# Weight-block sums moved from GpSimd instructions to accumulating DRAM-to-DRAM transfers, and some stores moved to ScalarE's queue

## The chip, the core and the metric

The kernel runs on one core of a Trainium2 chip. A core has five engines that each work through an instruction queue of their own, in order: TensorE (PE: matrix products into PSUM, with its weight loads PEld), VectorE (DVE), ScalarE (ACT), GpSimd (POOL) and SyncE (SP, which here only issues transfers). They meet through semaphores. Sixteen DMA engines move the data; a transfer is issued by an instruction on SP's, ACT's or POOL's queue. The metric is the device time of one execution in microseconds (us), lower is better.

## What is computed

One layer of a hybrid diffusion backbone in float32 over 1024 latent tokens of width 1024, with 256 context tokens. Cut to what matters here:

```python
hx = modulate(rmsnorm(x, norm1_g), sh1, sc1)
xq, xk, xv, xrq, xrk, xrv, xrg, xga, xgb = split(hx @ w_in)
o_na  = neighbourhood_attention(...)            # 8 heads of 64
o_ret = ret_output(bi_retention(...), xrg)      # 4 heads, chunks of 128, both directions
merged = sigmoid(xga) * (o_na @ w_proj_na) + sigmoid(xgb) * (o_ret @ w_proj_ret)
x = x + g1 * (merged @ w_out)
hx2 = modulate(rmsnorm(x, norm2_g), sh2, sc2)
u = depthwise_conv3(hx2 @ w_up) + conv_b        # w_up: 1024 x 5632
a, val = split(u)
x = x + g2 * ((silu(a) * val) @ w_down)         # w_down: 2816 x 1024
return rmsnorm(x, final_norm_g)
```

## The kernel before

Every float32 product is made of three TensorE products of halves: an operand is split into a rounded part (ACT, L86) and the rest (DVE, L87), and high*high, high*low and low*high are added in PSUM. So each weight block of 128x512 that arrives from DRAM passes through one ACT and one DVE instruction before TensorE may use it. The stages follow each other: start, neighbourhood attention (32 units, with pieces of projections and five plain gates between them), retention (4 heads of 10 slots, with three more plain gates at the end), the projection of the attention, the gates, `pret`, the output projection, the gated MLP's first product ("up"), its second ("down").

The gates, up and down are made by a scheme with seven block products in place of eight (class `Seven`, L1371 to L1431, and the loops of down). It needs sums and differences of the four 128x512 weight blocks of a unit, called s1 to s4. Three such sets exist:

- Gates and up: `Seven.load` (L1379) loads four blocks a21, a22, a11, a12 and lets POOL make s1 to s4 by four instructions (L1383 to L1386). In the up stage these eight tiles share a rotation of 12 buffers (`ur_load`, L1733; an earlier user of the same buffers is `comb`, which loads 16 tiles of the activation's sums). There are 22 up units; the first two are made plainly, the other 20 by the scheme. Unit i's seven steps are interleaved with its neighbours' (L1435): a unit takes seven steps' time, a step is 12 matmuls.
- Down: `down_sums` (L1238) is a generator that loads four w_down blocks on SP's queue into SBUF, subtracts on POOL (L1249) and stores the results to `d_w` in DRAM on SP's queue. It is advanced one subtraction at a time from the retention's slots, from the gates and from `pret`. 11 sets, 44 subtractions, 44 loads, 44 stores.

In a retention slot POOL also makes the rotated queries and keys (L1115: `r`), the low halves of the states (L1166: `SS`) and a power (L1193: `mvr`); all three feed TensorE by way of other engines. The retention's results leave by SP (`d_oret`, L1210), as do the plain gates (`d_gate`, L361). A store on SP's queue waits there for the ACT copy that fills its tile, and everything behind it on SP waits with it.

The order on each engine is set by the framework's list scheduler except where a part is written out by hand (the start, a piece of down's end); `late(...)` keeps marked instructions in the order of the program.

Of the kernel before, what the change touches and what calls it, by code (L numbers as in the profile page):

```python
# [8 lines left out]
F32 = mybir.dt.float32  # L9
# [7 lines left out]
P = 128  # L17
# [23 lines left out]
def tile_hybrid_layer(ctx, tc: tile.TileContext, io, dbg=None):  # L41
# [24 lines left out]
    edge = sb("edge", "right")  # L66
    cpool.tile([P, 24], F32, name="pad")
    edge.tile([P, 24], F32, name="pad")
# [467 lines left out]
    def ada_col2(i):  # L536
        w = ada2[i]
        late(vec.scalar_tensor_tensor(w, w, 1.0, cs2, ALU.mult, ALU.mult, accum_out=col[:, 16 + i : 17 + i]))  # L538
        if i + 1 < 32:
            ada_load()  # L540


    dec = cpool.tile([P, RH, 6], F32, name="dec")

# [468 lines left out]
    for i in range(NPAIR * NJ + 2):  # L1013
        live = i < NPAIR * NJ
        u1 = us[i - 1] if 1 <= i <= NPAIR * NJ else None
        u2 = us[i - 2] if i >= 2 else None
        if i == 0:
            ada_load()
        for n in (0, 1) if i == 1 else (i,) if 1 < i < 32 else ():
# [46 lines left out]
    class Head:  # L1066
# [129 lines left out]
        def mix_c(self, n):  # L1196
# [12 lines left out]
            if not end:  # L1209
                sync.dma_start(*stores.pop())  # L1210

# [23 lines left out]

    NH = NF // 2

    def down_sums(pool_, j0, j1, bufs=8):  # L1238
        def load(j, n):
            t = pool_.tile([P, 512], F32, tag="pj", bufs=bufs, name="pj")  # L1240
            sync.dma_start(t, io["w_down"][n % 2, NH * (n // 2) + j])
            return t

        ts, store = [load(j0, n) for n in range(4)], None
        yield
        for j in range(j0, j1):
            nxt = []
            for n, (c, x, y, o) in enumerate(((1, 1, 0, 0), (3, 3, 1, 1), (2, 3, 0, 3), (4, 2, 3, 2))):
                late(pool.tensor_tensor(ts[o], ts[x], ts[y], ALU.subtract))  # L1249
                if store:  # L1250
                    sync.dma_start(*store)
                store = (d_w[j, c - 1], ts[o])
                if j + 1 < j1:
                    nxt.append(load(j + 1, n))
                yield
            ts = nxt
        sync.dma_start(*store)

    RET_SUMS, GATE_SUMS = 5, 9
    ret_sums = down_sums(rt, 0, RET_SUMS)  # L1260
# [81 lines left out]
    def hx_sums(k):  # L1342
# [5 lines left out]
        b11, b12, b21, b22 = b[0, 0], b[0, 1], b[1, 0], b[1, 1]  # L1348
        for c, o, x, y in (("T1", b11, b12, b11), ("T3", b12, b22, b12), ("T2", b22, b22, b11), ("T4", b21, b21, b22)):
            late(vec.tensor_tensor(o, x, y, ALU.subtract))  # L1350
        yield
# [24 lines left out]
    class Seven:  # L1376
        loaded = False

        def load(self):  # L1379
# [3 lines left out]
            pool.tensor_tensor(self.s1, self.a21, self.a22, ALU.add)  # L1383
            pool.tensor_tensor(self.s2, self.s1, self.a11, ALU.subtract)
            pool.tensor_tensor(self.s3, self.a11, self.a21, ALU.subtract)
            pool.tensor_tensor(self.s4, self.a12, self.s2, ALU.subtract)  # L1386

# [8 lines left out]

        def add(self, b, half, bank, x):
            vec.tensor_tensor(self.dst(b, half), bank, x, ALU.add)
            self.done(b, half)

        def step(self, n):
# [7 lines left out]
            elif n == 1:  # L1409
                self.prod(self.Y, self.s2, "T2", True, False)  # L1410
                vec.tensor_tensor(self.u2, self.Y, self.p1, ALU.add)
            elif n == 2:
                self.prod(self.Z, self.s1, "T1", True, False)
            elif n == 3:
                self.fetch(1, 1)
                self.prod(self.Y, self.s3, "T3", False, False)
                vec.tensor_tensor(self.u3, self.Y, self.p1, ALU.add)  # L1417
                self.add(1, 1, self.Z, self.u3)
            elif n == 4:
# [3 lines left out]
            elif n == 5:  # L1423
                self.fetch(1, 0)
                self.prod(self.Y, self.a22, "T4", False, True)
                self.add(1, 0, self.Y, self.p1)
            else:
                self.fetch(0, 1)
                self.prod(self.Z, self.s4, "B22", False, True)
                self.add(0, 1, self.Z, self.u2)  # L1430

# [102 lines left out]

    gate_sums = down_sums(gr, RET_SUMS, GATE_SUMS)
    steps = interleaved(0, len(gu))
    n0, fetched = steps.index((len(gu) - 1, 0)), None
    for n, (i, k) in enumerate(steps):
        gu[i].step(k)
        if n % 3 == 1:  # L1540
            next(gate_sums, None)
        if fetched:
            orr_split(*fetched)
            fetched = None
        if n0 - KH - 1 <= n < n0 - 1:
            fetched = orr_load(wpool.tile([P, 512], F32, tag="raw", bufs=3, name="raw"), 0, n - n0 + KH + 1)
        elif n0 < n <= n0 + KH:
            fetched = orr_load(g_raw("orw"), 0, n - n0 - 1 + KH)

    def pret_load(db):  # L1550
        return [wload(io["w_pret"][db, i]) for i in range(2)]

    wp = {0: pret_load(0)}
    for _ in gate_sums:
        pass
    gr.release()
    tg.release()
# [25 lines left out]

    pjp = sb("out_sums", "right")
    out_sums = down_sums(pjp, GATE_SUMS, NH, 7)
    mg = {}

# [23 lines left out]
    for db in range(2, KB):  # L1611
# [4 lines left out]
        for half in range(2):  # L1616
            pret(db, half)
            next(out_sums, None)
    pjp.release()
    wo = {}  # L1620
# [39 lines left out]
    def norm_out(tb, xr):  # L1660
# [24 lines left out]
        (b11, b21), (b12, b22) = [(t[:, : KB // 2], t[:, KB // 2 :]) for t in (vo, vr)]  # L1685
        vec.tensor_tensor(b11, b12, b11, ALU.subtract)
        vec.tensor_tensor(b12, b22, b12, ALU.subtract)
        vec.tensor_tensor(b22, b22, b11, ALU.subtract)
        vec.tensor_tensor(b21, b21, b22, ALU.subtract)
# [64 lines left out]
    def conv(j, gate, value):  # L1754
# [18 lines left out]
        prev = {}  # L1773
        for c, x, y, o in ((S1, a21, a22, ALU.add), (S2, S1, a11, ALU.subtract), (S3, a11, a21, ALU.subtract), (S4, a12, S2, ALU.subtract)):
            x, y = (prev[v] if isinstance(v, int) else v for v in (x, y))
# [58 lines left out]

    seq = [j + NH * i for j in range(NH) for i in range(2)]
    PLAIN = 2

    for n, j in enumerate(seq[:PLAIN]):
# [8 lines left out]
        conv(j, *us2)  # L1847
    units = [Up(n, j) for n, j in enumerate(seq)]
    for i, n in interleaved(PLAIN, NF):
        units[i].step(n)  # L1850
    pu[1].release()
    pu[0].release()
# [84 lines left out]
    for b in range(QB):  # L1937
        pool.tensor_tensor(u2[b], u2[b], gate2[:, gs(1)], ALU.mult)
        pool.tensor_tensor(u2[b], u2[b], rows_of(b, 1), ALU.add)  # L1939

    steps(4, range(NH), True, False)
    for b in range(QB):
        x, z = rows_of(QB + b, 1), dw_tile("x2", NTB)
        part[QB + b, 1] = z
        vec.tensor_tensor(z, banks[0][b], u3[b], ALU.add)
        pool.tensor_tensor(z, z, gate2[:, gs(1)], ALU.mult)
# [140 lines left out]
```

## Time and profile before

| | us |
|---|---|
| three runs | 1764.68, 1762.41, 1764.07 (median 1764.07) |
| span of the profiled execution | 1759.2 |
| busy in it: PE, PEld, DVE, ACT, POOL | 1726.0, 1429.3, 1284.2, 849.2, 539.3 |
| POOL's L1249 (down's subtractions), 44 of them | 62.7 |
| POOL's L1383 to L1386 in up (20 units), 80 of them | 148.6 |

The span runs from the first to the last instruction of one profiled execution; that execution's own device time is not recorded beside it, so the 4.9 us between the span and the runs' median stand for what lies around the span. Busy time is the union of an engine's instructions. A matmul's record is longer than the distance between two starts (0.39 us against 0.23 us), so PE counts as busy where matmuls overlap, and what is idle on PE is a true stop. In the tables of waits a row reads: engine, tile and line that waited, what released it, us in total, how many times, the longest. In a timeline a row reads: start, length, engine, line, operation, output and inputs, count, and in brackets the idle time before it with what ended it.

### The profile page before, as it was taken

The page shows a single profiled execution, that of the slowest core. Times are in us where ns is not written, and L with a number is a line of the kernel's source. Part 1 is how long each engine was busy: PE and PEld are TensorE (multiplying, and loading weights), DVE is VectorE, ACT ScalarE, POOL GpSimd, SP SyncE. Part 2 cuts the span into 40 slices and gives each one's busy share as a digit, 9 for nine tenths or more (in the row PEclk, how much of TensorE's full clock was granted, in tenths as well). Part 3 has the DMA queues.
Part 4 walks back from the last instruction along what each step waited for, and adds up shares of the span by engine and source line. Part 5 has one row for each costly group of instructions (what it writes and reads, how often), then busy time and mean ns, then how long its engine had stood idle before and what let it go on. Part 6 is the DMA issues. An engine that isn't in the chain of part 4 may idle for free.

```text
span 1759.2 us, 24801 instructions
## 1 busy us (share of the span) xinstructions
PE 1726.0 (98%) x8405; PEld 1429.3 (81%) x8405; DVE 1284.2 (73%) x2454; ACT 849.2 (48%) x1826; POOL 539.3 (31%) x455
## 2 busy tenths in 40 slices
PE   8999999999999999999999999989999999999997
PEld 4688988888888888778888888778888888788886
DVE  4778887756776766777665557868899889875755
ACT  5666666653443434443444324534444444554444
POOL 1000000003334343555413300165555655211444
PEclk9999999999999999999999999999999999999999
DMA  9143334342231212677557733733322332586754
GB/s 348 61 130 125 95 117 147 117 133 87 73 108 43 72 42 68 203 238 239 200 199 268 246 143 132 254 108 102 108 90 92 118 120 90 170 296 192 239 162 162
DMA packets 139408, 261.10 MB, mean 148 GB/s; under 512 B 15856, under 2 KB 28304, under 8 KB 139280
## 3 DMA queue, kind: packets, MB, share of 16 engines
q1 hardware_dynamic: 139280, 259.51, 44.3%
q8 instruction: 66, 1.08, 0.3%
q14 instruction: 62, 0.51, 0.1%
HBM read 187.34 MB, written 69.48 MB: 146 GB/s over the span
## 4 chain that ended last, share of the span: by engine, by line
PE 43%; issue 6%; DVE 4%; POOL 3%; DMA 1%; ACT 1%; SPq 0%; POOLq 0%; ACTq 0%; DVEq 0%
PE u L1374 30%; PE y L1374 4%; PE pr L112 2%; PE pr L111 2%; PE pr L110 2%; PE om L122 1%; PE om L121 1%; PE om L123 1%; POOL x L1902 1%; DVE wc L87 0%; DVE b L1350 0%; DVE v L1679 0%; POOL pd L1939 0%; DVE hxT L87 0%; POOL x L1947 0%
## 5 line engine op out<-in xcount | busy, mean ns | idle before, releaser
L1374 PE MATMUL u<-T,wc 128*128 128x512 f32 x960 | 227.1, 392 | 5.1 <-ACT pu L1408 5.1
L1374 PEld LDWEIGHTS u<-T,wc 128*128 128x128 f32 x960 | 180.6, 189 | 45.7 <-ACT pu L1408 7.9
L1374 PE MATMUL y<-wc,ahl 128*128 128x512 f32 x924 | 210.6, 389 | 2.7 <-DVE wc L87 1.8
L1374 PEld LDWEIGHTS y<-wc,ahl 128*128 128x128 f32 x924 | 173.3, 188 | 39.7 <-DVE wc L87 2.5
L87 DVE TENSOR_TENSOR wc<-ur,wc 128x512 fp32r<-128x512 f32 x137 | 122.7, 897 | 65.8 <-ACT wc L86 65.8
L86 ACT CAST wc<-ur 128x512 fp32r<-128x512 f32 x137 | 85.0, 621 | 129.7 <-PE y L1374 72.3
L111 PE MATMUL mm<-low,wc 128*128 128x512 f32 (+1 forms) x328 | 124.0, 378 | 0.0
L1374 PE MATMUL u<-h2a,wc 128*128 128x512 f32 x480 | 112.3, 389 | 0.7 <-DVE pu L1417 0.7
L110 PE MATMUL mm<-hx,wc 128*128 128x512 f32 x264 | 107.4, 407 | 0.2 <-ACT wc L589 0.2
L1374 PEld LDWEIGHTS u<-h2a,wc 128*128 128x128 f32 x480 | 90.0, 188 | 19.8 <-DVE pu L1417 1.2
L112 PE MATMUL mm<-hx,wc 128*128 128x512 f32 x264 | 105.2, 399 | 0.0
L86 ACT CAST wc<-s 128x512 fp32r<-128x512 f32 x80 | 49.7, 623 | 93.2 <-PE u L1374 88.3
L123 PE MATMUL mm<-wc,low 128*128 128x512 f32 (+1 forms) x240 | 91.2, 380 | 0.0
L1374 PE MATMUL u<-hxT,wc 128*128 128x512 f32 x384 | 89.6, 389 | 0.0
L1508 POOL TENSOR_TENSOR col<-col,bcol 128x32 f32<-128x32 f32 x1 | 0.3, 253 | 280.7 <-DVE aw L538 280.7
L87 DVE TENSOR_TENSOR wc<-s,wc 128x512 fp32r<-128x512 f32 x80 | 83.5, 1046 | 3.8 <-ACT wc L86 3.4
L1374 PEld LDWEIGHTS u<-hxT,wc 128*128 128x128 f32 x384 | 72.1, 188 | 14.9
L87 DVE TENSOR_TENSOR wc<-raw,wc 128x512 fp32r<-128x512 f32 x92 | 68.0, 746 | 17.7 <-ACT wc L86 17.7
L121 PE MATMUL mm<-wc,hx 128*128 128x512 f32 x192 | 75.2, 392 | 0.6 <-ACT r L1105 0.6
L122 PE MATMUL mm<-wc,hx 128*128 128x512 f32 x192 | 75.2, 392 | 0.0
L1383 POOL TENSOR_TENSOR s<-ur 128x512 f32<-128x512 f32 x20 | 35.7, 1783 | 126.3 <-DVE wc L87 68.7
L86 ACT CAST wc<-raw 128x512 fp32r<-128x512 f32 x92 | 56.8, 621 | 33.0 <-PE pr L112 6.0
(393 smaller groups left out, 4671.3 us busy)
## 6 DMA issues: line engine op xcount, KB each, us to landing
ur<-in_w_up SPq DMA_DIRECT2D x80, 256.0 KB, 2.9
ur<-d_a SPq DMA_DIRECT2D x77, 256.0 KB, 3.1
aw<-in_w_ada SPq DMA_DIRECT2D x32, 512.0 KB, 3.3
pj<-in_w_down SPq DMA_DIRECT2D x44, 256.0 KB, 5.2
d_w<-pj SPq DMA_DIRECT2D x44, 256.0 KB, 2.0
d_a<-sa SPq DMA_DIRECT2D x44, 256.0 KB, 2.0
ur<-d_w SPq DMA_DIRECT2D x44, 256.0 KB, 3.8
d_a<-at SPq DMA_DIRECT2D x33, 256.0 KB, 2.7
```

What stands on the lines that cost most here:

```text
L86: act.copy(hi, src)
L87: (lo_eng or vec).tensor_tensor(lo, src, hi.bitcast(F32), ALU.subtract)
L110: pe.matmul(out, wh, xh, start=k == 0, stop=False)
L111: pe.matmul(out, wh, xl, start=False, stop=False)
L112: pe.matmul(out, wl, xh, start=False, stop=k == n - 1)
L121: pe.matmul(out, ah, bh, start=first, stop=False)
L122: pe.matmul(out, ah, bl, start=False, stop=False)
L123: pe.matmul(out, al, bh, start=False, stop=last)
L1374: pe.matmul(out, a, b, start=first and n == 0, stop=last and n == 2, skip_group_check=True)
L1383: pool.tensor_tensor(self.s1, self.a21, self.a22, ALU.add)
L1508: pool.tensor_tensor(col[:, 16:48], col[:, 16:48], bcol[:, 16:48], ALU.add)
L1902: pool.tensor_tensor(z, z, fg[:, gs(dh)], ALU.mult)
```

## The change

Weight sums are made by transfers within DRAM. A new generator `block_sums` issues, for each set, four plain copies of a block to DRAM (`copy_of`) and four transfers that add a block onto what already stands there (`sum_of`, `accum_op=ALU.add`), all on POOL's queue, in an order that puts copies and additions that depend on each other at least four transfers apart. [...] Where an operation only changes its sign or the order of its operands, its shape, engine and count stay.

- `up_jobs`: s1 to s4 of nine of the 20 up units (units 2 to 10) are made into `d_s`, 72 transfers, one per unit of attention (32) and one per slot of retention (40). Those up units now load seven blocks (four of them from `d_s`) in the order of use and issue nothing on POOL. The other 11 still make their sums on POOL.
- `down_jobs`: `d_w`'s 11 sets, 88 transfers: four sets in the gates (two transfers twice per unit), seven in up (the same, from unit 4 on). `down_sums`, its loads, subtractions and stores are gone, also from `pret`.
- Each step of issuing (`puts`) begins with a POOL copy of one column (128x1) from a tile of that step into a scratch cell `tick` (its name in the program is `pad`), which holds the transfer back until that tile is there: `st` in attention, `r0` in retention, u2 and u3 in gates and up.
- The stores `d_gate` of the eight plain gates (16) and `d_oret` of the retention (30, all but the last two) are issued on ACT's queue, behind the copy that fills their tile.
- The tile of attention's `aw` loads gets a second buffer.

```diff
+    d_s = dram.tile([9, 4, P, 512], F32, name="d_s")
...
-    cpool.tile([P, 24], F32, name="pad")
+    tick = cpool.tile([P, 24], F32, name="pad")[:, 0:1]
...
-            sync.dma_start(d_gate[db * 2 + br, half], t)
+            act.dma_start(d_gate[db * 2 + br, half], t)
...
-        w = na.tile([P, D], F32, tag="aw", bufs=1, name="aw")
+        w = na.tile([P, D], F32, tag="aw", bufs=2, name="aw")
...
+    NH, PLAIN, PRE, GATE_DOWN = NF // 2, 2, 9, 4
+    seq = [j + NH * i for j in range(NH) for i in range(2)]
+
+    def block_sums(jobs):
+
+        def add(out, src):
+            late(pool.dma_start(out, src, accum_op=ALU.add, max_dma_last_dim=8192))
+
+        def copy_of(n, c):
+            d, x, y, z, w = jobs[n]
+            late(pool.dma_start(d[c], (y, z, z, w)[c]))
+
+        def sum_of(n, c):
+            d, x, y, z, w = jobs[n]
+            add(d[c], (x, d[0], y, d[1])[c])
+
+        jobs = list(jobs)
+        for n in range(len(jobs) + 2):
+            for f, m, c in ((copy_of, n, 0), (sum_of, n - 1, 0), (copy_of, n, 2), (sum_of, n - 2, 3), (copy_of, n, 1), (sum_of, n - 1, 2), (copy_of, n, 3), (sum_of, n - 1, 1)):
+                if 0 <= m < len(jobs):
+                    yield f(m, c)
...
+    def puts(it, src, n):
+        late(pool.tensor_copy(tick, src))
+        for _ in range(n):
+            next(it, None)
...
+            puts(ret_sums, u1.st[:, 14:15], 1)
...
-                sync.dma_start(*stores.pop())
+                act.dma_start(*stores.pop())
...
-            if i < NCB + NTB - 3 and (head.h == 0 or i >= NCB):
-                next(ret_sums, None)
+            puts(ret_sums, head.r0[i][:, 1, 0:1], 1)
...
-        if n % 3 == 1:
-            next(gate_sums, None)
...
+        if k in (1, 3):
+            puts(gate_sums, (gu[i].u2 if k == 1 else gu[i].u3)[:, 0:1], 2)
...
-            next(out_sums, None)
...
+        def load(self):
+            n = self.n - PLAIN
+            if n >= PRE:
+                return super().load()
+            self.loaded = True
+            self.a11, self.s2, self.s1, self.s3, self.a12, self.a22, self.s4 = map(ur_load, (self.src[0, 0], d_s[n, 1], d_s[n, 0], d_s[n, 2], self.src[0, 1], self.src[1, 1], d_s[n, 3]))
...
+        if n in (1, 3) and i >= PLAIN + 2:
+            puts(up_sums, (units[i].u2 if n == 1 else units[i].u3)[:, 0:1], 2)
```

How the instructions move at the places of which the prediction speaks. First SP at the start of up: `ur<-d_t` are the 16 loads of `comb`, `ur<-in_w_up` the weight blocks of the first units of the scheme, `ur<-d_s` the ready sums, `d_a<-at` the store of the first finished activation. Before:

```order
L1735 DMA ur<-d_t 128x512 x11
L1735 DMA ur<-in_w_up 128x512 x4
L1766 DMA d_a<-at 128x512
L1735 DMA ur<-in_w_up 128x512 x8
L1771 DMA d_a<-at 128x512
```

and now:

```order
L1746 DMA ur<-d_t 128x512 x11
L1746 DMA ur<-in_w_up 128x512
L1746 DMA ur<-d_s 128x512 x3
L1746 DMA ur<-in_w_up 128x512
L1777 DMA d_a<-at 128x512
L1746 DMA ur<-in_w_up 128x512
L1746 DMA ur<-d_s 128x512
L1746 DMA ur<-in_w_up 128x512
```

The first unit's a11, s2, s1, s3, a12 now stand ahead of the store, its a22 and s4 and the next unit's a11 right behind it; before, the first unit's four blocks stood ahead of the store and the next unit's behind it.

At the same place ACT's queue, where `wc<-ur` and `wc<-s` are the rounded halves of weight blocks and of POOL's sums, `ta` and `at` belong to the convolution of the second plain unit, and `pu<-u` (L1408, now L1422) is the copy of the first product out of PSUM. Before:

```order
L1759 ACTIVATE ta<-u,cb,cw 128x1024
L86 CAST wc<-ur 128x512
L86 CAST wc<-s 128x512 x3
L86 CAST wc<-ur 128x512
L1762 ACTIVATE ta<-ta 128x1024
L1759 ACTIVATE at<-u,cb,cw 128x1024
L86 CAST wc<-ur 128x512
L1408 COPY pu<-u 128x512
```

and now:

```order
L87 CAST wc<-ur 128x512
L1770 ACTIVATE ta<-u,cb,cw 128x1024
L87 CAST wc<-ur 128x512 x4
L1773 ACTIVATE ta<-ta 128x1024
L1770 ACTIVATE at<-u,cb,cw 128x1024
L87 CAST wc<-ur 128x512
L1422 COPY pu<-u 128x512
```

The places in the queue are nearly the same; what the casts in front of the copy wait for is now a transfer where it was POOL.

Second, POOL in a slot of the retention's second head. Before:

```order
L1166 TENSOR_TENSOR SS<-st,SS 128x256
L1166 TENSOR_TENSOR SS<-run,SS 128x256
L1193 TENSOR_TENSOR mvr<-mvr,mhalf 128x1
L1115 TENSOR_TENSOR r_5491<-r_5491,r_5492 128x256
L1249 TENSOR_TENSOR pj<-pj 128x512
```

and now:

```order
L1207 TENSOR_TENSOR SS<-st,SS 128x256
L1207 TENSOR_TENSOR SS<-run,SS 128x256
L1234 TENSOR_TENSOR mvr<-mvr,mhalf 128x1
L1156 TENSOR_TENSOR r_5452<-r_5452,r_5453 128x256
L577 COPY pad<-r_5352 128x1
L550 DMA d_s<-in_w_up 32x2048
```

Where a subtraction of down stood between `r` and the next `SS`, there is now the one-column copy and one transfer, and this in every slot, where the subtractions stood in half of them.

More of the change, by code (lines that the diff above doesn't have):

```diff
@@ L538, in ada_col2, with up_jobs, down_jobs @@
         late(vec.scalar_tensor_tensor(w, w, 1.0, cs2, ALU.mult, ALU.mult, accum_out=col[:, 16 + i : 17 + i]))
-        if i + 1 < 32:
+        if i + 2 < 32:
             ada_load()
+    NH, PLAIN, PRE, GATE_DOWN = NF // 2, 2, 9, 4
[14 more added lines that the diff above has]
+                    yield f(m, c)
+    def up_jobs():
+        for n in range(PRE):
+            a = {(b, i): io["w_up"][seq[PLAIN + n], b, i] for b in range(2) for i in range(2)}
+            yield [d_s[n, c] for c in range(4)], a[1, 1], a[1, 0], a[0, 0], a[0, 1]
+    def down_jobs(j0, j1):
+        for j in range(j0, j1):
+            b = {(r, c): io["w_down"][c, NH * r + j] for r in range(2) for c in range(2)}
+            yield [d_w[j, c] for c in range(4)], b[0, 0], b[0, 1], b[1, 1], b[1, 0]
+    def puts(it, src, n):
+        late(pool.tensor_copy(tick, src))
+        for _ in range(n):
+            next(it, None)
+    ret_sums = block_sums(up_jobs())
     dec = cpool.tile([P, RH, 6], F32, name="dec")
@@ L1233, in done @@
             return self.n >= NTB + 2
[L1236 to L1260, printed above, removed]
     def slot(main, mix, head=None, i=None):
@@ L1348, in hx_sums @@
         b11, b12, b21, b22 = b[0, 0], b[0, 1], b[1, 0], b[1, 1]
-        for c, o, x, y in (("T1", b11, b12, b11), ("T3", b12, b22, b12), ("T2", b22, b22, b11), ("T4", b21, b21, b22)):
-            late(vec.tensor_tensor(o, x, y, ALU.subtract))
+        for o, x, y, op in ((b11, b11, b12, ALU.subtract), (b12, b12, b22, ALU.subtract), (b22, b22, b11, ALU.add), (b21, b21, b22, ALU.subtract)):
+            late(vec.tensor_tensor(o, x, y, op))
         yield
@@ L1773, in conv @@
         prev = {}
[L1774 removed]
+        for c, x, y, o in ((S1, a21, a22, ALU.subtract), (S2, S1, a11, ALU.subtract), (S3, a11, a21, ALU.subtract), (S4, a12, S2, ALU.add)):
             x, y = (prev[v] if isinstance(v, int) else v for v in (x, y))
```

54 lines of the change are left out of this document (26 added, 28 removed).

## The prediction, made before the changed kernel had run

> **What bounds the kernel now.** I read the page's first part, then busy time by stage, then PE's waits. The windows are attention, retention, the gates, `pret`, the first steps of up's scheme and the rest of up; the columns are the stretch, its length, busy PE, PEld, DVE, ACT and POOL, the granted clock, the DMA engines' share and GB/s.
>
> ```profile
> span 1759.2 us, 24801 instructions
> PE 1726.0 (98%) x8405; PEld 1429.3 (81%) x8405; DVE 1284.2 (73%) x2454; ACT 849.2 (48%) x1826; POOL 539.3 (31%) x455
> ```
>
> ```profile
> 95.00:390.00 295.00, 294.77 (x1827) 259.37 (x1827) 225.32 (x634) 188.68 (x557) 0.70 (x3) 1.00 0.38 119
> 390.00:713.00 323.00, 321.69 (x1691) 274.25 (x1690) 221.72 (x706) 133.50 (x383) 115.04 (x150) 1.00 0.26 81
> 769.00:915.00 146.00, 146.00 (x646) 120.92 (x645) 96.79 (x122) 60.40 (x103) 62.13 (x42) 1.00 0.66 220
> 915.00:1020.00 105.00, 105.00 (x465) 86.92 (x464) 55.18 (x81) 39.21 (x67) 29.92 (x22) 1.00 0.75 253
> 1147.00:1166.00 19.00, 13.85 (x55) 11.02 (x54) 12.18 (x13) 7.28 (x12) 14.07 (x10) 0.91 0.47 153
> 1166.00:1534.00 368.00, 367.25 (x1613) 301.92 (x1612) 325.44 (x330) 168.76 (x235) 191.54 (x109) 1.00 0.33 109
> ```
>
> TensorE is the bound. Of 1759.2 us it is idle for 33, and in five of these six stretches, 1237 us long, it misses 0.23 + 1.31 + 0 + 0 + 0.75 = 2.3 us at a granted clock of 1.00. The work that the change moves lies behind PE there, and to move it wins nothing. The change can win only where PE truly stops, and the fifth stretch has such a place: 13.85 of 19 us. The list of PE's waits names it:
>
> ```profile
> PE u L1374 <- ACT pu L1408: 5.1, 1, 5.1
> PE y L1374 <- DVE wc L87: 1.8, 2, 1.4
> PE y L1374 <- ACT wc L86: 0.9, 1, 0.9
> PE u L1374 <- DVE pu L1417: 0.7, 1, 0.7
> PE mm L122 <- DVE wx L87: 0.7, 3, 0.2
> PE mm L121 <- ACT r L1105: 0.6, 1, 0.6
> ```
>
> **Term 1, the stop at the start of up.** The timelines of PE, ACT, POOL, SP and DVE around it (start, length, what; in brackets the idle time before and what ended it):
>
> ```profile
> 1147.63 2.88 PE L1374 MATMUL u<-h2a,wc 128*128 128x512 f32 x12
> 1150.35 1.07 PE L1374 MATMUL u<-T,wc 128*128 128x512 f32 x4
> 1156.57 5.69 PE L1374 MATMUL u<-T,wc 128*128 128x512 f32 x17 [5.15 <-ACT pu L1408]
> ```
>
> ```profile
> 1152.85 0.62 ACT L86 CAST wc<-ur 128x512 fp32r<-128x512 f32 x1 [4.21 <-DMA ur<-in_w_up]
> 1155.93 0.58 ACT L1408 COPY pu<-u 128x512 f32<-128x512 f32 x1
> ```
>
> ```profile
> 1146.70 1.29 POOL L1385 TENSOR_TENSOR s<-ur 128x512 f32<-128x512 f32 x1
> ```
>
> ```profile
> 1133.35 2.47 SPq L1735 DMA_DIRECT2D ur<-in_w_up  x4
> 1140.20 0.33 SPq L1766 DMA_DIRECT2D d_a<-at  x1
> 1148.02 10.13 SPq L1735 DMA_DIRECT2D ur<-in_w_up  x8
> ```
>
> ```profile
> 1140.10 3.69 DVE L87 TENSOR_TENSOR T<-ur,T 128x512 fp32r<-128x512 f32 x6
> ```
>
> ```profile
> ur<-in_w_up SPq DMA_DIRECT2D x80, 256.0 KB, 2.9
> ```
>
> PE's second product may start when ACT has copied the first (`pu`) out of PSUM. The first product ends at 1150.5, the copy takes 0.58, the four matmuls in between end at 1151.4: with ACT free, PE would have lost nothing. But on ACT's queue the copy stands behind a cast that starts only at 1152.85, because its block came late: SP went on loading at 1148.02, when POOL's third sum (1146.70 + 1.29 = 1147.99) had let go of a buffer. The 5.15 us hang on the chain of POOL's sums, a buffer, SP, a load and ACT.
>
> The change takes POOL out of this chain. The unit's sums come from `d_s`, written hundreds of us earlier, and the loads stand in the order of use. The next unit's first block, which the same cast will need, then waits for the store at 1140.20 and for the twelfth of `comb`'s sixteen buffers. The row of DVE shows the last six being freed in 3.69 us, the twelfth by 1141.4. SP issues three loads behind the store, at 2.47/4 = 0.62 us each, so by 1142, and the load lands 2.9 us later, near 1145. ACT has the casts of s2, s1 and s3 (0.62 each) to do until then, and the copy's turn is at 1150.5: 5 us of room. Bounds: 5.15 won if all of that room holds, nothing if a buffer is late all the same. I take 4.7, near the upper end, since the row that named POOL as the releaser is the nearest.
>
> **Term 2, POOL.** Removed: 44 subtractions of down and, in nine up units, 36 sums; added: 124 one-column copies and 160 transfers to issue. POOL's busy time on the tiles `s` in up, and on `sa` (stretch, length, busy, count, clock, DMA):
>
> ```profile
> L1249 POOL TENSOR_TENSOR pj<-pj 128x512 f32<-128x512 f32 x44 | 62.7, 1426 | 7.5 <-DMA pj<-in_w_down 7.0
> 1166.00:1534.00 368.00, 130.88 (x71) 1.00 0.33 109
> 1166.00:1534.00 368.00, 60.73 (x38) 1.00 0.33 109
> ```
>
> 63 us and 36 x 130.88/71 = 66 us leave POOL, and bring nothing elsewhere, since PE stood still for none of it. What a POOL-issued transfer costs POOL, call it p with its copy, no row shows. The nearest below is SP's 0.33 us for issuing the store at 1140.20, the nearest above the 1.43 us subtraction that it replaces; I take 1.3, as POOL's own rows are nearer. A retention slot has room for it:
>
> ```profile
> 564.04 1.30 POOL L1249 TENSOR_TENSOR pj<-pj 128x512 f32<-128x512 f32 x1
> 567.09 0.74 POOL L1166 TENSOR_TENSOR SS<-st,SS 128x256 fp32r<-128x256 f32 x1 [1.74 <-ACT SS L1165]
> ```
>
> The transfer takes the subtraction's place and 1.74 us of waiting follow, so p is free up to 3.0, in every slot. In up a unit takes 19.0 us (84 matmuls at (2.88 - 1.07)/8 = 0.226). Units 11 to 17 have on POOL four sums (7.4), half of the four `sa` (3.2) and 4p: full at p = 2.1. Yet their sums run early:
>
> ```profile
> 1354.82 1.29 POOL L1384 TENSOR_TENSOR s<-s,ur 128x512 f32<-128x512 f32 x1 [3.14 <-issue]
> 1381.39 4.83 PE L1374 MATMUL u<-T,wc 128*128 128x512 f32 x20
> ```
>
> The second sum ends 25 us before its product starts, so seven units' lag of 4(p - 2.1) each stays hidden up to p = 3.0. Cost: 0.
>
> [...]
>
> **Term 3, ScalarE's queue.** 46 stores move to ACT. At SP's 0.39 us ACT spends 18 us more in 618 us of attention and retention, where it is busy for 322. In a slot:
>
> ```profile
> 701.33 0.39 SPq L1210 DMA_DIRECT2D d_oret<-ot  x1
> ```
>
> ```profile
> 567.50 0.38 ACT L1207 COPY ot<-tpo 128x256 f32<-128x256 f32 x1
> 568.83 0.37 ACT L1100 CAST v<-mm 128x256 fp32r<-128x256 f32 x1 [0.95 <-PE mm L123]
> ```
>
> The store follows the copy at 567.50, where 0.95 us of idle time cover it. Bounds: nothing, or 18 us if PE met every one. PE's waits in these stages are pieces of 0.2 and one of 0.6 (`mm` above); I put two more of 0.2, 0.4 us. The scheduler also orders attention and retention anew: at most their 1.5 us of idle time can be won by that, and I allow as much lost; 0 in the sum.
>
> **Term 4, transfers.**
>
> ```profile
> q1 hardware_dynamic: 139280, 259.51, 44.3%
> ```
>
> 44.3% of the span for 259.5 MB is 0.79 us of all 16 engines for 256 KB that pass once. A copy within DRAM is one to two passes, an addition one to three. In up 56 transfers over 14 units (266 us) and 27 more loads make 65 to 131 us: from 0.33 to between 0.58 and 0.82 busy. In the gates 32 transfers replace 32, at most 38 us of 146 more: 0.66 to at most 0.92. `pret` ran at 0.75 with PE busy for 105.00 of 105.00, so up to there it costs nothing; with two passes for each transfer both stages come to about 0.75, which I take.
>
> The sum: 1759.2 - 4.7 + 0.4 = 1754.9 of span; with the 4.9 us by which the runs' median exceeds the span, **1759.8 us**, 0.24% below 1764.07. About 0.2% (3.5 us) is what a measurement of this kernel tells from no change: faster means below 1760.5, slower above 1767.6.
>
> **Rivals.** (a) The stop stays, for another reason: the next unit's block still waits, for a buffer or for the store. For it: the last of `comb`'s buffers come free only at 1143.8, and one late load holds ACT's whole queue. Against it: the releaser was POOL. 1762 to 1765. (b) More is won: the waits of 2.7 us for `wc` in down and 0.7 for `pu` at up's end go too, as VectorE no longer shares its time with POOL's sums, and the new order wins its 1.5. 1755 to 1757. (c) Slower: issuing holds POOL for more than 3.0 us. Then `SS` and behind it `r` are late in each of 40 retention slots; at p = 3.4 that is 16 us, less the gain: 1776. Against it: p would be nine times SP's 0.33. (d) Slower: in the gates the engines go past 0.75 busy and a unit's blocks arrive after their turn; at 1 to 2 us for each of eight units, 1768 to 1776. (e) Slower: half of retention's 30 stores on ACT meet PE: 6 us, 1766.
>
> **Chances.** Forecast 0.46 (1757.5 to 1761.5 by itself), (a) 0.20, (b) 0.09, (c) 0.11, (d) 0.08, (e) 0.06. Below 1760.5 lie some 0.38 of the forecast and all of (b): faster 0.47. Within: the forecast's rest, most of (a), and part of (e): 0.28. Slower: (c), (d) and what is left of (a) and (e): 0.25. The range reaches down past (b) and up into (c) and (d): 1754 to 1771.
>
> **What would show it.** Right: PE's 5.1 us wait on `pu` is gone or under 1 us, PE's busy share in attention and retention stays within 1 us, and POOL holds each transfer for less than 3 us. Wrong: that wait stands there under another name (a); PE waits in retention for `qk` or `SS` (c); PE waits in the gates for `wc` or `o` at a DMA share over 0.75 (d); PE waits for an ACT copy behind a store (e).

## The result, and the profile after

| | before | changed |
|---|---|---|
| median of five runs each, us | 1764.68 | 1771.09 |
| lowest and highest, us | 1762.41, 1766.02 | 1769.79, 1775.01 |
| span of the profiled execution, us | 1759.2 | 1769.3 |

The change makes the kernel slower by 0.45%: the ratio is 1.0045, with an interval of 1.0032 to 1.0057. The prediction said 1759.8 and faster; the time lies just above its range.

The first profile of the kernel before was of a quick execution. A second one, taken beside the experiments, has a span of 1763.0 and a device time of 1764.76, and its stages are the ones to compare with. So 1.8 us lie around a span, as in the changed kernel (1771.09 and 1769.3); of the 4.9 us that stand for this ahead of the prediction, the other 3.1 belong to the quick execution. Stages are bounded here by TensorE's matmuls: attention from the first `ptp` to the first `dS`, the retention to the last `dS`, the gates from their first to their last `u`, up from its first to its last `u`. First the windows of the second profile of before (attention, retention, gates, up; the columns are those of the windows in the prediction):

```profile
112.50:393.60 281.10, 280.22 (x1730) 245.91 (x1729) 217.16 (x617) 181.88 (x542) 0.70 (x3) 1.00 0.39 120
393.60:672.20 278.60, 277.64 (x1467) 237.74 (x1467) 196.88 (x632) 115.91 (x334) 97.15 (x125) 1.00 0.24 75
770.20:922.40 152.20, 152.20 (x673) 126.06 (x672) 100.70 (x127) 63.76 (x108) 62.41 (x42) 1.00 0.67 221
1103.40:1541.70 438.30, 431.95 (x1888) 354.14 (x1887) 384.45 (x424) 203.89 (x295) 212.79 (x121) 0.99 0.38 124
```

The same four of the changed kernel:

```profile
112.10:394.20 282.10, 281.03 (x1731) 245.19 (x1730) 217.09 (x618) 181.86 (x544) 26.11 (x67) 1.00 0.49 148
394.20:676.90 282.70, 278.68 (x1465) 237.53 (x1464) 190.19 (x631) 115.93 (x331) 105.70 (x183) 1.00 0.29 73
774.60:934.30 159.70, 154.00 (x674) 127.10 (x673) 94.78 (x127) 63.61 (x108) 66.36 (x74) 0.98 0.70 208
1115.30:1547.70 432.40, 429.42 (x1888) 352.25 (x1887) 367.51 (x424) 203.89 (x295) 205.13 (x177) 1.00 0.56 177
```

The stage lengths give the account: attention +1.0, retention +4.1, gates +7.5, up -5.9. That is +6.7, the rest of the program together -0.4, against 6.3 between these two spans and 6.4 between the medians. The gain that the change was to bring is there, and two stages in which TensorE hardly stopped before have lost twice as much. TensorE's waits name the places (the row of the old stop on `ACT pu` is now the last of these):

```profile
PE u L1388 <- DVE pu L1431: 7.2, 3, 5.7
...
PE dS L124 <- DVE kz L1176: 2.3, 4, 0.8
...
PE u L1388 <- ACT pu L1422: 0.5, 3, 0.2
```

**The gates.** One stop of 5.70 us, at the end of their last unit. The timelines of SyncE, ScalarE, VectorE and TensorE around it; `orw<-d_orr` are loads for the next stage, `orr<-orw` their split:

```profile
908.51 1.34 SPq L1541 DMA_DIRECT2D orw<-d_orr  x2
914.84 0.62 ACT L87 CAST orr<-orw 128x512 fp32r<-128x512 f32 x1 [5.94 <-DMA orw<-d_orr]
917.99 0.62 ACT L87 CAST orr<-orw 128x512 fp32r<-128x512 f32 x1 [2.53 <-DMA orw<-d_orr]
919.69 0.32 SPq L1496 DMA_DIRECT2D d_gate<-c  x1
920.11 0.88 SPq L1541 DMA_DIRECT2D orw<-d_orr  x2
926.64 0.69 DVE L1431 TENSOR_TENSOR pu<-u,pu 128x512 f32<-128x512 f32 x1
927.47 2.90 PE L1388 MATMUL u<-hxT,wc 128*128 128x512 f32 x6 [5.70 <-DVE pu L1431]
```

TensorE waits for `pu`, VectorE stands behind the split of a load, ScalarE idles 5.94 and 2.53 us for two loads, so the sigmoid that `d_gate<-c` stores is late, and behind that store on SyncE are the next two loads. Before, SyncE issued all four loads in one piece, ahead of that store (the second profile):

```profile
903.47 1.93 SPq L1527 DMA_DIRECT2D orw<-d_orr  x4
907.74 1.36 ACT L86 CAST orr<-orw 128x512 fp32r<-128x512 f32 x2 [3.23 <-DMA orw<-d_orr]
910.71 0.32 SPq L1482 DMA_DIRECT2D d_gate<-c  x1
```

The changed program has one more edit here, which the account of the change leaves out: its loop holds two of these loads before it splits the first, where it was one. e10, below, has the old loop and the new order all the same.

And the loads are slow: the casts of the first two begin 6.3 and 9.5 us behind the first issue, where the first two of before begin 4.3 us behind it. The DMA engines are full just then; of four windows of 3 us from 903 to 915, with shares of 0.91 to 1.11, the first and the last:

```profile
903.00:906.00 3.00, 3.00 (x15) 2.46 (x14) 1.43 (x3) 1.53 (x3) 2.03 (x3) 1.00 0.91 302
912.00:915.00 3.00, 3.00 (x15) 2.49 (x14) 0.00 (x0) 0.17 (x1) 0.00 (x0) 1.00 1.11 379
```

The share alone does not make the difference, though. In the second profile of before the same place stands at 0.90 to 0.97 for 9 us, from 900 to 909, and TensorE does not stop:

```profile
900.00:903.00 3.00, 3.00 (x15) 2.48 (x14) 1.92 (x4) 2.59 (x5) 0.00 (x0) 1.00 0.97 364
903.00:906.00 3.00, 3.00 (x15) 2.49 (x14) 2.05 (x4) 0.62 (x1) 0.00 (x0) 1.00 0.90 268
```

Over the whole stage the share is 0.70, hardly more than the 0.67 of before. That the transfers slow these loads is shown by e1, which leaves them out.

**The retention.** Where heads change, POOL now issues a transfer just as VectorE begins `kz`; POOL, VectorE and TensorE of the changed kernel:

```profile
531.27 0.81 POOL L550 DMA_DIRECT2D d_s<-in_w_up  x1 [0.25 <-issue]
531.34 2.60 DVE L1176 SCALAR_TENSOR_TENSOR kz<-r,dec,kz 128x128 fp32r<-128x128 f32 x2 [0.28 <-ACT kz L1175]
531.88 0.97 POOL L1207 TENSOR_TENSOR SS<-st,SS 128x256 fp32r<-128x256 f32 x1
532.58 0.94 POOL L1207 TENSOR_TENSOR SS<-run,SS 128x256 fp32r<-128x256 f32 x1
533.74 0.38 PE L124 MATMUL dS<-v,kz 128*128 128x256 f32 x1 [0.85 <-DVE kz L1176]
```

and the same place before:

```profile
527.78 0.74 POOL L1166 TENSOR_TENSOR SS<-st,SS 128x256 fp32r<-128x256 f32 x1 [5.06 <-DVE o L1181]
528.04 0.89 DVE L1135 SCALAR_TENSOR_TENSOR kz<-r,dec,kz 128x128 fp32r<-128x128 f32 x2 [0.28 <-ACT kz L1134]
...
528.67 0.86 POOL L1166 TENSOR_TENSOR SS<-run,SS 128x256 fp32r<-128x256 f32 x1
```

Before, the first `SS` ran early and 0.15 us of pause followed, in which `kz` got through. Now the first `SS` starts only when the transfer has been issued; by then the second is ready too, and the two run without a pause. The first of the pair of `kz` ends, as before, 0.15 us behind POOL's work: it takes 2.34 us, to 533.68, and POOL's ends at 533.52. In the first profile of before 20 `kz` run beside a subtraction of down, take 0.92 to 0.98 us in place of 0.35, and they too end 0.15 us behind it. The issuing alone does not do this: 34 of the 72 `kz` of the changed kernel run while POOL issues a transfer and does nothing else, most of them from 0.4 us into it, and they take 342 to 354 ns. Nor does an issue with two `SS` behind it do it every time. At the third change of heads in e4, which has the same program here but for the stores' queue, the second `kz` starts 0.06 us behind the issue, as one of 2.35 us does in the changed kernel, and takes 0.35 us (VectorE, then POOL):

```profile
608.85 0.64 DVE L1176 SCALAR_TENSOR_TENSOR kz<-r,dec,kz 128x128 fp32r<-128x128 f32 x2 [0.28 <-ACT kz L1175]
609.08 0.80 POOL L550 DMA_DIRECT2D d_s<-d_s  x1 [0.56 <-issue]
609.68 0.97 POOL L1207 TENSOR_TENSOR SS<-st,SS 128x256 fp32r<-128x256 f32 x1
610.38 0.96 POOL L1207 TENSOR_TENSOR SS<-run,SS 128x256 fp32r<-128x256 f32 x1
```

In e1 it is the same. By the records the first `SS` starts 0.53 and 0.54 us behind the start of the two longest `kz`, which alone would take 0.35. So `kz` is held for over 1 us only where `SS` follow an issue closely, but what decides there, and what holds it until the first `SS` starts, stays open.

**Up's start.** TensorE's second product follows the first without a stop:

```profile
1161.67 2.88 PE L1388 MATMUL u<-h2a,wc 128*128 128x512 f32 x12
...
1164.39 3.89 PE L1388 MATMUL u<-T,wc 128*128 128x512 f32 x16
1164.59 0.59 ACT L1422 COPY pu<-u 128x512 f32<-128x512 f32 x1 [0.99 <-PE u L1388]
```

### The profile page after: what moved, and what is told of

Read it like the earlier page. It is cut to its first block, busy times and chain, and to the rows that moved or that the text cites. A ratio compares the mean times of both kernels' runs of the same rounds, so it can differ in the third digit from the quotient of the medians.

```text
span 1769.3 us, 25014 instructions
## 1 busy us (share of the span) xinstructions
PE 1729.0 (98%) x8405; PEld 1428.8 (81%) x8405; DVE 1257.6 (71%) x2454; ACT 849.2 (48%) x1826; POOL 560.9 (32%) x659
## 3 DMA queue, kind: packets, MB, share of 16 engines
q0 software_dynamic: 6400, 41.95, 10.7%
## 4 chain that ended last, share of the span: by engine, by line
PE 42%; issue 6%; DVE 4%; POOL 4%; ACT 1%; DMA 1%; SPq 0%; POOLq 0%; ACTq 0%; DVEq 0%
PE u L1388 25%; PE y L1388 4%; PE om L123 2%; PE om L122 2%; PE om L124 2%; PE pr L111 2%; PE pr L113 2%; PE pr L112 2%; DVE wc L88 1%; PE u L112 1%; PE u L113 1%; PE u L111 1%; POOL x L1920 1%; DMA o<-d_pn 0%; DVE at L1771 0%
## 5 line engine op out<-in xcount | busy, mean ns | idle before, releaser
L88 DVE TENSOR_TENSOR wc<-ur,wc 128x512 fp32r<-128x512 f32 x173 | 144.0, 836 | 72.5 <-ACT wc L87 72.4
L87 ACT CAST wc<-ur 128x512 fp32r<-128x512 f32 x173 | 107.3, 622 | 164.2 <-PE u L1388 86.3
L577 POOL COPY pad<-st 128x1 f32<-128x1 f32 x32 | 5.9, 183 | 249.1 <-DVE st L486 249.1
L1788 POOL TENSOR_TENSOR sa<-at 128x512 f32<-128x512 f32 x22 | 37.7, 1716 | 127.6 <-DVE at L1774 114.2
L577 POOL COPY pad<-pu 128x1 f32<-128x1 f32 x52 | 36.2, 696 | 108.9 <-DVE pu L1425 62.0
L112 PEld LDWEIGHTS mm<-low,wc 128*128 128x128 f32 x328 | 62.1, 189 | 6.8
```

Source lines behind the costliest of these rows:

```text
L87: act.copy(hi, src)
L88: (lo_eng or vec).tensor_tensor(lo, src, hi.bitcast(F32), ALU.subtract)
L112: pe.matmul(out, wh, xl, start=False, stop=False)
L577: late(pool.tensor_copy(tick, src))
L1788: pool.tensor_tensor(prev[c], x, y, o)
```

## The experiments

In the table are the lengths of four stages in one profiled execution each, and the ratio to runs of the kernel before on the same chip. All kernels compute the same function; "changed" is the starting point of e1 to e5, e8 and e9. The gates have the same program in changed, e3, e4, e8 and e9 and lie between 157.3 and 159.7, up has the same in changed and e4 and differs by 2.2: with the transfers in, differences of 2 us in these two stages are scatter.

| | attention | retention | gates | up | ratio, interval |
|---|---|---|---|---|---|
| before, first profile | 281.0 | 278.3 | 152.2 | 437.8 | |
| before, second (e0) | 281.2 | 278.6 | 152.2 | 438.3 | 0.9998, 0.9987 to 1.0009 |
| changed | 282.1 | 282.7 | 159.7 | 432.4 | 1.0045, 1.0032 to 1.0057 |
| e1: no transfers in the gates, more in up | 282.1 | 286.0 | 154.3 | 436.1 | 1.0043, 1.0030 to 1.0055 |
| e3: none in the retention | 282.3 | 278.1 | 157.3 | 435.8 | 1.0006, 0.9997 to 1.0016 |
| e4: stores back on SyncE | 281.9 | 282.2 | 157.4 | 434.6 | 1.0039, 1.0025 to 1.0053 |
| e5: e1 and e3 together | 282.2 | 278.2 | 153.6 | 441.3 | 1.0022, 1.0012 to 1.0033 |
| e8: one-column copies alone in the retention | 282.1 | 278.5 | 158.6 | 434.1 | 1.0026, 1.0015 to 1.0037 |
| e9: no transfers where heads change | 282.1 | 280.2 | 157.4 | 432.3 | 1.0023, 1.0010 to 1.0036 |
| e6, four units: what pays, alone | 281.5 | 279.3 | 152.2 | 430.9 | 0.9961, 0.9946 to 0.9975 |
| e6, two units | 281.5 | 278.9 | 152.2 | 430.6 | 0.9969, 0.9958 to 0.9980 |
| e10: e6 and the gates' transfers | 281.4 | 278.6 | 159.7 | 431.5 | 1.0002, 0.9992 to 1.0012 |

### e1: the gates without transfers

```diff
-    gate_sums = block_sums(down_jobs(0, GATE_DOWN))
...
-        if k in (1, 3):
-            puts(gate_sums, (gu[i].u2 if k == 1 else gu[i].u3)[:, 0:1], 2)
...
-    up_sums = block_sums(down_jobs(GATE_DOWN, NH))
+    up_sums = block_sums(down_jobs(0, NH))
...
-            puts(up_sums, (units[i].u2 if n == 1 else units[i].u3)[:, 0:1], 2)
+            puts(up_sums, (units[i].u2 if n == 1 else units[i].u3)[:, 0:1], 3)
```

> The gates issue no transfers; all 88 of down are issued in up, three instead of two at each step. SyncE's order of loads and stores in the gates is that of the changed kernel. Theory 1 (the gates' transfers crowd the DMA engines, so that the loads of orw arrive after their turn): PE's stop of 5.70 us on pu (DVE L1431) at 921 falls under 1 us, the span loses about 5.7 us, the time stands at 1.0013 of the kernel before instead of 1.0045. Rival (the changed order on SyncE, two loads of orw behind the store of a gate, makes the stop): it stays, 1.0045. Third possibility (half as many transfers again in up are too many there): the stop goes, but new stops in up take the gain, 1.004 or more.

Both theories had a part. The stop shrinks from 5.70 to 1.88 us, and the gates from 159.7 to 154.3, not to 152.2. The rest goes with the order on SyncE, which is the changed kernel's here too, though no run puts back that order alone (SyncE, ScalarE and TensorE):

```profile
912.52 1.07 SPq L1541 DMA_DIRECT2D orw<-d_orr  x2
916.82 1.27 ACT L87 CAST orr<-orw 128x512 fp32r<-128x512 f32 x2 [3.71 <-DMA orw<-d_orr]
919.45 0.32 SPq L1496 DMA_DIRECT2D d_gate<-c  x1
919.87 0.88 SPq L1541 DMA_DIRECT2D orw<-d_orr  x2
...
927.87 2.52 PE L1388 MATMUL u<-hxT,wc 128*128 128x512 f32 x10 [1.88 <-DVE pu L1431]
```

The casts of the first two loads now begin 4.3 us behind the first issue, as before the change, where it was 6.3 and 9.5; the last two loads stand behind the store as in the changed kernel. The time did not fall, and the third possibility says why in part: up is 3.7 us longer. The rest is the retention, 286.0 against 282.7 with the same program there: in this execution a weight block of `wx` came late, TensorE stopped for 2.23 us, and 3.2 us at half clock followed, which cost another 1.6:

```profile
605.80 0.69 PE L122 MATMUL mm<-wx,hc 128*128 128x384 f32 x1 [2.23 <-ACT wx L87]
```

```profile
605.60:607.20 1.60, 1.40 (x6) 1.41 (x6) 0.69 (x1) 0.14 (x1) 0.00 (x0) 0.50 0.24 90
```

By so much this stage can differ from one execution to the next; whether the transfers had a part in that block's delay is not shown.

### e3, e4: the retention

e3 takes the transfers out of the retention, e4 takes the stores off ScalarE's queue.

```diff
-    NH, PLAIN, PRE, GATE_DOWN = NF // 2, 2, 9, 4
+    NH, PLAIN, PRE, GATE_DOWN = NF // 2, 2, 4, 4
...
-            puts(ret_sums, head.r0[i][:, 1, 0:1], 1)
```

> Four units instead of nine get their sums from transfers, all 32 issued in attention; the retention issues none, and five more units of up make theirs on POOL. Theory 2 (in the retention the issuing holds POOL, POOL's work closes up behind it and keeps VectorE out, so that kz and with it dS come late): PE's waits for kz fall from 2.3 us to under 0.7, no kz lasts over 1 us, the retention is 3 to 4.7 us shorter, 1.002 to 1.003 of the kernel before. Rival (the stores on ScalarE's queue make the retention longer): the retention is within 1 us of the changed kernel's, 1.0045. In up both expect no new stop, since the sums of those units run ahead of their products.

```diff
-            act.dma_start(d_gate[db * 2 + br, half], t)
+            sync.dma_start(d_gate[db * 2 + br, half], t)
...
-                act.dma_start(*stores.pop())
+                sync.dma_start(*stores.pop())
```

> The 16 stores of the plain gates and the 30 of the retention go back to SyncE's queue, nothing else. Theory 2: no gain, within 1 us of the changed kernel, 1.0040 to 1.0050, since kz waits for POOL and not for ScalarE. Rival (stores on ScalarE's queue): attention and retention get 3 to 6 us shorter, 1.001 to 1.003.

Without transfers the retention lasts 278.1 us, the 278.6 of before, and TensorE no longer waits for `kz`. With the stores on SyncE it lasts 282.2. The transfers make the loss, the stores nothing that can be seen. In up e3 is longer than the changed kernel by 3.4 us, but than e4 by 1.2 only. Five more units sum on POOL there, beside the 56 transfers that up issues; that may no longer be free, against what both theories expected, but it is not shown. The time fell further than forecast, to 1.0006 against 1.002 to 1.003; the stages of the one profile do not show why.

### e5: both, and the price moves to up

The edits of e1 and e3 together.

> The edits of the two runs before together: transfers in attention (32) and in up (88) alone. Theories 1 and 2 together: the losses of 5.7 and 3 to 4.7 us go, the gain at up's start stays, so 0.997 to 0.9995 of the kernel before (1759 to 1764 us). If either theory is wrong, the time stays at 1.001 to 1.003; if transfers in up cost time, above that.

The retention (278.2) and the gates (153.6) came back as forecast, yet the time did not: up lasts 441.3 us, 3 more than before, although its first stop is gone. Sixteen units sum on POOL beside 88 transfers, and VectorE and POOL look as in the retention. POOL:

```profile
1336.25 1.11 POOL L550 DMA_DIRECT2D d_w<-in_w_down  x1
1336.80 1.89 POOL L1396 TENSOR_TENSOR s<-ur 128x512 f32<-128x512 f32 x1
```

and VectorE:

```profile
1337.47 1.77 DVE L88 TENSOR_TENSOR wc<-s,wc 128x512 fp32r<-128x512 f32 x1
...
1339.17 2.31 DVE L1765 SCALAR_TENSOR_TENSOR ta<-uu,cw,ta 128x1023 f32<-128x1023 f32 x1
1341.40 0.68 DVE L1430 TENSOR_TENSOR pu<-u,pu 128x512 f32<-128x512 f32 x1
```

VectorE's subtraction takes 1.77 us beside POOL's sums (the longest of before takes as much) and 0.68 without; what follows is `pu`, and here TensorE waits 1.00 us for it, in five such places 0.5 to 1.0 each. That the transfers close POOL's work up into such trains is my reading of these rows; what the runs show is the length of up by what is in it: no transfers and 16 or 18 units summed on POOL 430.6 to 431.5, 56 transfers and 11 or 12 units 432.3 to 434.6, 56 and 16 units 434.1 to 435.8, 88 and 11 units 436.1, 88 and 16 units 441.3.

### e8, e9: what in the retention costs

e8 keeps `puts` in every slot of the retention but leaves nothing for it to issue (only the first line of e3's diff); e9 leaves `puts` out of the two context slots of each head:

```diff
-    NH, PLAIN, PRE, GATE_DOWN = NF // 2, 2, 9, 4
+    NH, PLAIN, PRE, GATE_DOWN = NF // 2, 2, 8, 4
...
-            puts(ret_sums, head.r0[i][:, 1, 0:1], 1)
+            if i >= NCB:
+                puts(ret_sums, head.r0[i][:, 1, 0:1], 1)
```

> Four units from transfers, all issued in attention, as in the run with an empty retention; but the retention's 40 one-column copies stay, without transfers behind them. Theory (what holds POOL is the issuing): the retention lasts 278 to 279.5 us, 1.0006 to 1.001 of the kernel before. Rival (the copies, which wait for r on POOL's queue, make it late): it lasts 281 or more, 1.002 to 1.003.

> The changed kernel without transfers in the retention's two context slots of each head (8 of the 40 slots); 32 transfers stay in the others, and eight units instead of nine get their sums that way. Theory (the loss comes where issuing and two SS in a row close up and keep VectorE from kz, which is at the change of heads alone): no kz over 1.2 us, the retention lasts 279 to 280 us instead of 282.7, 1.002 to 1.003. Rival (every transfer in the retention costs its share): 32/40 of the loss stays, 281.8 us, 1.0037 or more.

The copies cost the retention nothing (278.5). Its time as a whole is higher than the theory's: 1.0026, with an interval that touches that of e3 at its end; no stage of its profile shows from where, and that stays open. In e9, `kz` by itself (VectorE; in the row least, median and most ns; in the changed kernel the most is 2347):

```profile
L1176 DVE SCALAR_TENSOR_TENSOR kz<-r,dec,kz x72: 339/352/1111, 390.9 to 670.7; 128x128 fp32r<-128x128 f32 x72
```

The eight slots at the change of heads carried 282.7 - 280.2 = 2.5 of the 4.1 us, as the theory said of the greater part, though it had forecast 279 to 280; 1.6 us lie in the other 32 slots, where no single wait over 0.4 us is left to point at.

### e0, e6: what pays, alone

e0 is the kernel before once more. e6 starts from the changed kernel, takes down's sums back to POOL in the retention, the gates and `pret` (by `down_sums`, with additions, since the changed kernel makes the sums of weights with plus and has the minus in the sums of activations and in later combinations), the stores back to SyncE, `aw` to one buffer and the gates' loop to its old form, and issues transfers in attention alone, for the first four units of up that need sums, or for two.

```diff
-    NH, PLAIN, PRE, GATE_DOWN = NF // 2, 2, 9, 4
+    NH, PLAIN, PRE = NF // 2, 2, 4
...
+                late(pool.tensor_tensor(ts[o], ts[x], ts[y], ALU.add))
...
-            puts(ret_sums, head.r0[i][:, 1, 0:1], 1)
+            if i < NCB + NTB - 3 and (head.h == 0 or i >= NCB):
+                next(ret_downs, None)
...
-        if k in (1, 3):
-            puts(gate_sums, (gu[i].u2 if k == 1 else gu[i].u3)[:, 0:1], 2)
+        if n % 3 == 1:
+            next(gate_sums, None)
```

> The kernel before once more, for the scatter of its stages from one profiled execution to the next: ratio 1.000 within 0.001, stages within 1 us of the first profile, the 5.15 us stop at up's start in it again, and behind it some 3 us at a granted clock of 0.50.

> Only what pays is kept: the sums of up's first four seven-product units come from 32 transfers issued in attention; down's sums are subtractions' mirror images on POOL at their old places (additions, signs as in the changed kernel), the stores are on SyncE again, aw has one buffer, the loop of the gates is the old one. My theories (attention loses about 1 us, the retention and gates lose nothing, up's start wins its stop of 5.15 and the 1.7 that PE takes to come back to full clock): 1764.7 + 1 - 6.9, 0.9965 of the kernel before (0.9955 to 0.9975). Rival (the gain at up's start is eaten by transfers in attention or by late loads): 0.999 to 1.001.

> The version that keeps what pays, with two units instead of four from transfers (16 in attention). Theory (the gain is the stop at the very start of up): the stop stays away, up lasts 430.5 to 432 us, 0.9955 to 0.997 of the kernel before. Rival (the gain is POOL's lighter load in all of up): 1 to 3 us of it are lost, 0.9975 or more.

e0 repeats the stages within 0.5 us and has the stop, 4.9 us this time. e6 is faster than both kernels: 0.9961 with four units, 0.9969 with two, the intervals overlapping. Up lasts 430.9 and 430.6, so two units suffice: the gain is the stop at the start with the half clock behind it, and POOL's lighter load in the rest of up brings nothing that can be told.

### e10: the gates alone

```diff
-    gate_sums = down_sums(gr, RET_SUMS, GATE_SUMS)
+    gate_sums = block_sums(down_jobs(RET_SUMS, GATE_SUMS))
...
-        if n % 3 == 1:
-            next(gate_sums, None)
+        if k in (1, 3):
+            puts(gate_sums, (gu[i].u2 if k == 1 else gu[i].u3)[:, 0:1], 2)
```

> The version that keeps what pays, and on top of it the gates alone as in the changed kernel: four sets of down by 32 transfers in the gates in place of 16 subtractions with their loads and stores. Theory (the changed order on SyncE costs 1 to 2 us, the transfers' share of the DMA engines 2 to 4 more, and a stop of over 3 us another 1.7 at half clock): the gates last 156 to 160 us instead of 152.2, 0.9985 to 1.0005 of the kernel before. Rival (it was the sum of the changes up to there that made the gates long): within 1 us of 152.2, 0.996.

159.7 us, as in the changed kernel, and the whole of e6's gain is given back by this one edit. That the two agree to 0.1 us is chance: here the stop is 4.47 us and 5.8 us at half clock follow, there it is 5.70 and 3.2. What the gates lost came from the gates' own transfers and the order that goes with them: SyncE issues two loads, the store and two loads here too, although the loop is the old one.

## Why the prediction was wrong, step by step

**Term 1 was right, and too small.** The 5.1 us wait on `pu` is gone, by the path that was described. But the term counted the stop alone. Behind it TensorE starts again at half speed (the second profile of before, where the stop ends at 1158.2; the column of the clock is the one before the DMA engines' share):

```profile
1158.20:1159.80 1.60, 1.60 (x4) 1.31 (x5) 1.60 (x3) 0.46 (x1) 1.03 (x1) 0.50 0.42 129
...
1161.40:1163.00 1.60, 1.60 (x5) 1.27 (x4) 1.31 (x2) 0.00 (x0) 0.99 (x1) 0.50 0.33 125
1163.00:1164.60 1.60, 1.60 (x8) 1.29 (x7) 1.13 (x2) 0.62 (x1) 1.60 (x2) 1.00 0.66 247
```

4.8 us at a granted clock of 0.50 cost 2.4 more. The rows that the prediction quoted for 1147 to 1166 had it in them: a clock of 0.91 in that stretch. In place of -4.7 the stop was worth -7.4 (438.3 to 430.9 in e6), of which the changed kernel kept 5.9; its up, with 56 transfers in it, is 1.5 longer than e6's.

**Term 2 was right in p and wrong in what p pays for.** Issuing a transfer holds POOL for 0.75 us on the mean of all 160. With the copy's 0.30 in the retention that is near 1.05, below the 1.3 taken. The step that failed is "p is free up to 3.0, in every slot". The room was read from one slot in the middle of a head and called every slot's; and it was reckoned on POOL, from the start of `SS` to the time when `SS` is needed, while the cost fell on VectorE, whose `kz` took up to 2.35 us beside POOL's issue and `SS` in place of 0.35. POOL's arithmetic had held `kz` up in the kernel before too (0.92 to 0.98 us beside a subtraction), at no cost there to TensorE; now TensorE waits for `kz` in four places, 2.3 us in all, and e9 puts 2.5 of the 4.1 us on the changes of heads. In up the length went with transfers and sums together (e5), and the rows there speak for the same hold of POOL on VectorE; that it is this is not shown.

How POOL holds `kz` up is not shown: the 2.35 us of the changed kernel began before the first `SS`, and in e1 and e4 the same sequence held nothing.

**Term 3 was right** in the stores: on ScalarE they cost nothing that can be told (e4). The 1.0 us that attention lost is more than the 0.4 allowed, and its cause stays open; it is 0.7 with the stores on SyncE (e4) and 0.2 to 0.3 with `aw` in one buffer as well (e6, e10).

**Term 4 was near in the gates' share and wrong in the conclusion.** The share was to be about 0.75 in both stages and is 0.70 in the gates and 0.56 in up. By the prediction's own figures two passes for each transfer make 0.83 in the gates (0.66, and 32 x 0.79 us more in 146), not 0.75; the slip did not show, since a transfer took fewer: a transfer within DRAM costs 1.18 us of all engines (10.7% of 1769.3 us over 160) against 0.79 for a simple pass:

```profile
q0 software_dynamic: 6400, 41.95, 10.7%
```

The bounds that the prediction took, one to two passes for a copy and one to three for an addition, hold but for the shortest copies: in the changed kernel's attention, reckoned from each issue to the next one, the 19 copies take 0.62 to 1.36 us of all engines, 0.8 to 1.7 passes, and the 13 additions 1.38 to 2.20, 1.7 to 2.8 passes. Two windows of 10 us, one with a copy (from 160) and one with an addition (from 179):

```profile
q0 software_dynamic: 32, 0.26, 6.7%
...
q0 software_dynamic: 48, 0.26, 16.6%
```

The step that failed: "`pret` ran at 0.75 with PE busy for 105.00 of 105.00, so up to there it costs nothing". A mean over 150 us says nothing of the few loads on which a queue stands, and a stage that stands a full share in its own order is no measure for another, in which ScalarE's queue stands on loads for the next stage. Rival (d) had the right place and half of the mechanism, late loads, at a chance of 0.08; that its 1768 to 1776 holds the measured time is in part luck, since it looked for eight waits on `wc` or `o` at a share above 0.75 and one came, by way of `orw`, at 0.70, with the retention's loss and up's gain beside it. What no rival had: with POOL's sums, their loads and stores gone SyncE's order changed too, so that two of four loads fell behind a store. The prediction weighed the order at the start of up alone. In e1 and e5, without transfers, the stop is 1.2 to 1.9 us; with them it is 3.2 to 5.7, and the half clock behind it, 3.2 us in the changed kernel and 5.8 in e10, costs another 1.6 and 2.9.

**The sum by measured sizes**, from the second profile of before: 1763.0 + 1.0 (attention) + 4.1 + 7.5 - 5.9 = 1769.7, and 1769.3 was found. These are differences between two profiles, so they add up by themselves; what the experiments support is where they belong. The chances went wrong with them: (c) and (d) were priced as accidents that exclude each other, and both stages lost at once. Of (c) only the stage came true: p is near 1.05 and not above 3.0, and TensorE waited for `kz`, not for `qk` or `SS`.

## What to carry to other kernels

Work that is moved off a busy engine into stages where the bound engine never stops can only lose there; keep of such a change the part that removes a stop, here the 16 transfers of two units, and leave the rest where it was. Ask of added work not only whether its own engine has room, but whether it closes up the pauses in which a neighbour gets through (0.15 us for `kz` before the change), and judge DMA load by how late the loads come on which an in-order queue stands, not by the mean of the stage: a share of 0.90 to 0.97 for 9 us did no harm before. The stops of 2.23, 4.47, 4.90 and 5.70 us cost TensorE 1.6 to 2.9 us more than their length, one of 1.88 us nothing more. Before calling an edit local, compare the order of every queue in the stages where it removes something.

## What the hardware showed that I had not expected

- After a stop of 2.23 us (e1, in the retention), 3.24 (e3), 4.90 (before) and 5.70 (changed), TensorE's granted clock is 0.50 for 3.2 to 4.8 us; after one of 1.88 (e1, in the gates) it is 1.00 at once. The longer stop does not have the longer way back: behind the 4.47 us of e10, which end at 920.67, it is 5.8 us, the longest seen here (windows of e10):

```profile
923.80:925.40 1.60, 1.60 (x5) 1.31 (x4) 0.40 (x1) 0.00 (x0) 0.00 (x0) 0.50 0.77 186
925.40:927.00 1.60, 1.60 (x6) 1.22 (x6) 0.82 (x2) 0.72 (x2) 0.00 (x0) 0.66 0.91 305
```

  A stop of 2.23 us was enough for the half clock here and one of 1.88 was not; what parts these two no run here shows.
- While POOL issues a transfer and does nothing else, VectorE's `kz` keeps its 0.35 us (34 cases in the changed kernel). Even 0.06 us into an issue with two `SS` behind it, it was held for 2.35 us in the changed kernel and not at all in e1 and e4.
